# A hybrid encoder layer: the first output product of the attention beside the second pair's scores, and one k-tile in another order in three blocks

## The chip, the cores and the metric

The kernel runs on one core of a Trainium2 chip. A core has engines that work side by side, each with its own stream of instructions, and that wait for each other through semaphores: TensorE (PE in the profile; its weight loads are listed apart as PEld), VectorE (DVE), ScalarE (ACT), GpSimd (POOL), and SyncE (SP), which here only issues transfers. The metric is the device time of one execution in microseconds. A change of about 0.2% is what a measurement of this kernel can tell from none.

## What is computed

One layer of an encoder on a sequence of 256 tokens with a model width of 2048, all in 32-bit floats:

```python
hn = _rmsnorm(h, norm_w[i])
proj = hn @ w_in[i]
q, v, f_fwd, f_bwd, z_a, b_gate, c_gate, h_b, z_b = jnp.split(proj, IN_SPLITS, axis=-1)
o_a = _hgrn2_bidirectional(jax.nn.silu(q), v, f_fwd, f_bwd, lb_all[:, i])
o_a = _head_rmsnorm(o_a, hgrn_norm_w[i]) * jax.nn.silu(z_a)
y_b = b_gate * _short_conv(c_gate * h_b, conv_w[i])
o_b = _rmsnorm(y_b, conv_norm_w[i]) * jax.nn.silu(z_b)
h = h + jnp.concatenate([o_a, o_b], axis=-1) @ w_out[i]
gate = jax.nn.sigmoid(h @ w_ple_gate[i])
h = h + (p[i] @ w_ple[i]) * gate
return _rmsnorm(h, final_norm_w)
```

`_hgrn2_bidirectional` is a gated linear attention with 16 heads of 128, in chunks of 64 tokens, once forwards and once backwards: scores from `q` and `k`, masked, times `v`, with a decayed state carried from chunk to chunk.

## The kernel before

**Precision.** Each 32-bit operand is split into a high part in a faster format (`spl[..., 0]`, cast by ScalarE at L101) and the remainder (`spl[..., 1]`, subtracted by VectorE at L102). A product is then high x high, high x low and low x high. For the weights the two parts come from `Stream.split`, which runs three parts ahead of TensorE; a part holds four k-tiles of a block of 256 output columns, or less of a wider one. The weights arrive by transfers from SP into a ring of raw buffers.

**A block of the input projection.** `gemm_in(c, i, orders)` (L408) multiplies one block of 256 columns (two row tiles `m` of the transposed result) in 16 k-tiles. In one k-tile `gemm_part` (L393) issues four matmuls: for each `m` a long one (L403), whose moving operand has 512 columns, the high and the low part of the input side by side, against the weights' high part, and a short one (L401) with 256 columns against the weights' low part. The order is a table of pairs (m, short). `PLAIN` is long, short, long, short. `orders` gives single k-tiles another order: `SHORTS` is short, short, long, long, and `OUTER` is long, short, short, long. `ONE` puts `SHORTS` at k-tile 1, and `BOTH` puts `OUTER` at k-tile 1 and `SHORTS` at k-tile 5. All orders issue the same four matmuls.

**Ticks.** Each k-tile ends with `tick()` (L330), which counts up and runs what is due. `at(dt, fn)` (L297) puts `fn` in `dt` ticks from now. So work of the attention is issued between the k-tiles of projection blocks, on all engines at that place of the program. One block of `gemm_in` is 16 ticks.

**The attention half.** `two_pairs(i)` (L788) runs for i = 0, 2, 4, 6. Each call works on two pairs of heads, i and i + 1. It runs six blocks, `B_FF`, `B_FB` and `B_Q` for pair i and then for pair i + 1; then `gemm_vz` (L432), a product with 512 moving columns in every matmul, which gives `v` and `z` for both pairs (pair 0 uses the plainer `gemm_two`). `kicks` (L822) says which of the six blocks gets an order of its own. Four ticks into `gemm_vz` come the scores of pair i. What is put in after `gemm_vz` falls into the next call's first three blocks: the preparation of pair i + 1 at tick 4, `out(0)` at tick 12, the scores of pair i + 1 at tick 32 (at the end of the second block), `out(1)` at tick 46. In the first call, i = 0, `out(0)` and the scores of pair 1 are put in at one tick, in this order (L850, L851). After the last call, i = 6, the next blocks are those of the convolution half: `B_CG`, `B_HB` and `B_BG` of its loop (L901).

**What these steps issue.** The scores are 80 small matmuls (L711) and 8 of 128 columns (L755), then copies on VectorE and ScalarE and sums on POOL. `out(e)` (L842) calls `outputs` (L765): 16 matmuls as the profile counts them (L773, L774) into one PSUM bank (`o`, tag `y`), four squares with accumulated sums on ScalarE (L778) and one copy on VectorE (L779) into `ogz`, which `finish_two` reads at least 24 ticks behind the third block. `out(1)` uses the same bank as `out(0)`.

**The convolution half.** Eight rounds of four blocks (`B_CG`, `B_HB`, `B_BG`, `B_ZB`), all in plain order but for `B_BG` of round 0, which has `BOTH`. Meanwhile the output projection's weights are read and added up by transfers (`pump`). Then come the output projection and the gated embedding.

Of the kernel before, what the change touches and what calls it, by code (L numbers as in the profile page):

```python
# [25 lines left out]
B_Q, B_V, B_FF, B_FB, B_ZA, B_BG, B_CG, B_HB, B_ZB = (8 * i for i in range(9))  # L26
# [89 lines left out]
def tile_hymba_encoder(  # L116
# [180 lines left out]
    def at(dt, fn):  # L297
        pend.append((now[0] + dt, len(pend), fn))
# [91 lines left out]
    ONE = {1: SHORTS}  # L390
# [17 lines left out]
    def gemm_in(c, i, orders={}):  # L408

        acc = acc_in(c, i)  # L410
        for g in range(4):
            gemm_part(acc, ws.get(blocks[c, i][g]), g, orders=orders)
        return acc
# [374 lines left out]
    def two_pairs(i):  # L788
        vt = ap_.tile([P, 2, 512], F32, tag="vt", name=f"vt{i}")
        zt = ap_.tile([P, 2, 512], F32, tag="zt", name=f"zt{i}")  # L790
        ss = ap_.tile([P, 2, 2, 2], F32, tag="ss", name=f"ss{i}", bufs=2)
        ogs, steps, forgets = [], [], []
        before = last_two[0]
        if i == 6:
            for z in range(4):
                at(10 + 10 * z, lambda z=z: prepare(prepared[z]))
        else:


            todo = vz_prepared[i + 2]  # L800
            for z, what in enumerate(todo):
                at(50 + 10 * z, lambda what=what: prepare(what))
                for step in range(3):

                    dt = (166, 196, 220)[step] + z if i else 98 + 6 * step + z
                    at(dt, lambda what=what, step=step: add_up(what, step))
        if i == 2:

            def xsums(z):
                k = 2 * VZ_SUMS[z]  # L810
                a, t = xq[1][:, 0].rearrange("p (k t) -> p k t", k=2), xq[1][:, 1].rearrange("p (o t) -> p o t", o=4)
                act_sums(xs[:, k : k + 2], a, t)
                act_split(xq[0][:, z], xs[:, k : k + 2], t)

            for z in range(len(VZ_SUMS)):
                at(10 + 12 * z, lambda z=z: xsums(z))
        for e in range(2):
            xf = ap_.tile([P, 2, 2, T], F32, tag="xf", name=f"xf{i + e}", bufs=2)
            qt = ap_.tile([P, 2, T], F32, tag="qt", name=f"qt{i + e}")
            first3 = i + e == 0  # L820

            kicks = {(0, 1): ({}, ONE, BOTH), (2, 0): (ONE, BOTH, {}), (4, 0): ({}, {}, BOTH), (6, 0): ({}, {}, BOTH)}  # L822
            kick = kicks.get((i, e), ({}, {}, BOTH if i + e else {}))
            for j, (c, dst) in enumerate(((B_FF, xf[:, 0]), (B_FB, xf[:, 1]), (B_Q, qt))):

                acc, offset = acc3[j] if first3 else gemm_in(c, i + e, kick[j]), 500 if e and j == 2 else 200
                evac(acc, lambda m, dst=dst: dst[:, m, :], ap_, offset)

            def mix(e=e, xf=xf, qt=qt):
                forgets.append((xf, qt, mix_forgets(i + e, xf, qt)))  # L830
                if e == 0:
                    if before:
                        before()
                    steps.append(mix_pair(i, *forgets[0]))

            if first3:

                at(15, mix)
            else:
                mix()  # L840

        def out(e):  # L842
            ogs.append(ap_.tile([P, 2, 2, P], F32, tag="ogz", name=f"ogz{i + e}", bufs=2))
            steps[e][1](vt, ogs[e], ss[:, e])

        if i == 0:

            at(18, lambda: steps[0][0]())
            at(19, lambda: steps.append(mix_pair(i + 1, *forgets[1])))
            at(46, lambda: out(0))  # L850
            at(46, lambda: steps[1][0]())  # L851
            at(60, lambda: out(1))
            gemm_two(B_V, i, vt)
            xctx.close()
            xqp = xqctx.enter_context(tc.tile_pool(name="xqp", bufs=1, side="left", reuse_waits="tile"))
            xq.append(xqp.tile([P, len(VZ_SUMS), 4, 2, P], F32R, name="xsum"))
            xq.append(xqp.tile([P, 2, 512], F32, name="xd"))
            gemm_two(B_ZA, i, zt)
        else:

            at(4, lambda: steps[0][0]())
            gemm_vz(i, vt, zt)
            at(4, lambda: steps.append(mix_pair(i + 1, *forgets[1], here=True)))
            at(12, lambda: out(0))
            at(32, lambda: steps[1][0]())
            at(46, lambda: out(1))

        def rest():
            gate_two(i, zt)
            if i < 6:  # L870
                at(24, lambda: finish_two(ogs, ss, zt, ogs))
                for e in range(2):
                    at(32, lambda e=e: turn(i + e, ogs[e], "yx"[e]))
            else:

                def keep():
                    kept.extend(psm.tile([P, 2, 2, P], F32, tag=f"sc{e}", name=f"kept{e}") for e in range(2))
                    finish_two(ogs, ss, zt, kept)

                at(50, keep)  # L880

        last_two[0] = rest
# [17 lines left out]
    pool.memset(ysum, 0.0)  # L900
    for i in range(8):  # L901
        cg = ctmp.tile([P, 2, T], F32, tag="cg", name=f"cg{i}", bufs=2)
        evac(gemm_in(B_CG, i), lambda m: cg[:, m, :], ctmp)
        hb = ctmp.tile([P, 2, T], F32, tag="hb", name=f"hb{i}", bufs=2)
        evac(gemm_in(B_HB, i), lambda m: hb[:, m, :], ctmp)
        u = ub[i % 2]
        by_norms(cg, rbc2, 2)
        pump()
        pool.tensor_tensor(out=u[:, :, 1 : T + 1], in0=cg, in1=hb, op=ALU.mult)
        pump()  # L910
        for m in range(2):
            ct = 2 * i + m
            dve.tensor_scalar(cg[:, m, :], u[:, m, 0:T], cvw[:, 0, ct : ct + 1], None, op0=ALU.mult)
            for j in (1, 2):
                dve.scalar_tensor_tensor(
                    out=cg[:, m, :], in0=u[:, m, j : j + T], scalar=cvw[:, j, ct : ct + 1],
                    in1=cg[:, m, :], op0=ALU.mult, op1=ALU.add,
                )
        evac(gemm_in(B_BG, i, {} if i else BOTH), lambda m: hb[:, m, :], ctmp)
        pool.tensor_tensor(out=cg, in0=cg, in1=hb, op=ALU.mult)  # L920
        pump()
        y2 = ctmp.tile([P, 2, T], F32, tag="tmp", name=f"y2_{i}")
        act.activation(y2, cg, AF.Square)
        pool.tensor_tensor(out=ysum, in0=ysum, in1=y2, op=ALU.add)
        pump()
        evac(gemm_in(B_ZB, i), lambda m: hb[:, m, :], ctmp)
        by_norms(hb, rbc, 2)
        pump()
        sz = ctmp.tile([P, 2, T], F32, tag="tmp", name=f"szb{i}")
        act.activation(sz, hb, AF.Sigmoid)  # L930
        for m in range(2):
            ct = 2 * i + m
            dve.scalar_tensor_tensor(
                out=hb[:, m, :], in0=hb[:, m, :], scalar=cnw[:, ct : ct + 1], in1=sz[:, m, :],
                op0=ALU.mult, op1=ALU.mult,
            )
        pool.tensor_tensor(out=cg, in0=cg, in1=hb, op=ALU.mult)
        pump()
        if i == 0:
            assert not pend  # L940
            actx.close()
            bp = mctx.enter_context(tc.tile_pool(name="bp", bufs=1, side="right", reuse_waits="tile"))
            mixb = bp.tile([P, NH, 2, T], F32R, name="mixb")
            og = bp.tile([P, 2, 2, 2, P], F32, name="og")
            suma = bp.tile([P, len(SUMS), 3, 2, P], F32R, name="suma")
        if i == 2:
            for e in range(2):
                act.copy(out=og[:, e], in_=kept[e])
        hi, lo = mixb[:, 2 * i : 2 * i + 2, 0, :], mixb[:, 2 * i : 2 * i + 2, 1, :]
        act.copy(out=hi, in_=cg)  # L950
        dve.tensor_tensor(out=lo, in0=cg, in1=hi, op=ALU.subtract)
        for src, z, n in ((mixa, i - 1, len(SUMS)), (mixb, i - SUMS[0], len(sumb32))):
            if 0 <= z < n:
                k = 2 * SUMS[z]
                a = ctmp.tile([P, 2, T], F32, tag="tmp", name=f"sa{i}")
                if src is mixb:
                    act_sums(mixb[:, k : k + 2], a, sumb32[z])
                else:
                    t = ctmp.tile([P, 4, P], F32, tag="hb", name=f"sb{i}", bufs=2)
                    act_sums(mixa[:, k : k + 2], a, t)  # L960
                    act_split(suma[:, z], mixa[:, k : k + 2], t)
# [281 lines left out]
```

## Time and profile before

| | |
|---|---|
| runs | 1114.24, 1115.87, 1116.77 us (median 1115.87) |
| span of the profiled execution, first to last instruction | 1115.1 us |
| the profiled execution's own time | not given; its span lies within the runs |
| long matmuls (L403), 128x512 | 1792, mean length 395 ns |
| short matmuls (L401), 128x256 | 1792, mean length 280 ns |

The page gives the busy time of each engine, the span in 40 slices, the chain of work that ended last, and groups of instructions. Matmuls are pipelined: the length of one (395 ns) is longer than the distance to the next, so the rate is read from the starts of the rows in the timeline, not from the lengths. The timeline's rows give start, length, engine, line, operation, tiles and shape; a row with x3 merges three equal instructions in succession. In brackets stands the idle time of the engine before the row, and what ended it. The windows view gives, for a stretch, the busy time and the number of instructions of each engine, the granted clock of TensorE, the share of time that the transfer engines were busy, and GB/s. Pieces of the chain are start, length and what ran.

### The profile page before, as it was taken

How to read it: one execution, taken by the hardware profiler on the slowest of the kernel's cores; microseconds unless marked ns; L12 is line 12 of the kernel's file. 1: busy time of each engine (PE TensorE's matmuls, PEld its weight loads, DVE VectorE, ACT ScalarE, POOL GpSimd, SP SyncE). 2: the span in 40 equal slices, each digit the busy share in tenths (PEclk: the TensorE clock that was granted, in tenths of full speed). 3: DMA queues.
4: the chain of work that ended last, by engine and by line, in shares of the span. 5: the costliest groups of instructions: out<-in, count | busy, mean ns of one | idle time of the engine just before them, and what ended most of it. 6: DMA issues, size and time to landing. Idle time of an engine off the chain costs nothing.

```text
span 1115.1 us, 16970 instructions
## 1 busy us (share of the span) xinstructions
PE 1105.0 (99%) x6464; PEld 951.2 (85%) x6464; DVE 826.7 (74%) x1088; ACT 671.6 (60%) x939; POOL 291.5 (26%) x239
## 2 busy tenths in 40 slices
PE   9999999999999999999999999999999999999997
PEld 8888888888888888888888888888888888888886
DVE  7899467786887778797658748855758878877673
ACT  6787567666875697565535534534446565565562
POOL 1045325105530525043333223423331000000101
PEclk9999999999999999999999999999999999999998
DMA  9775985668778966858999998999979987887532
GB/s 348 273 249 192 223 266 179 217 227 213 234 207 306 303 172 182 279 180 206 296 312 252 263 335 218 294 311 266 298 201 296 332 287 284 297 305 254 196 132 76
DMA packets 79121, 277.76 MB, mean 249 GB/s; under 512 B 7872, under 2 KB 22080, under 8 KB 60736
## 3 DMA queue, kind: packets, MB, share of 16 engines
q1 hardware_dynamic: 64800, 253.26, 65.3%
q0 software_dynamic: 13952, 23.07, 13.6%
q8 instruction: 51, 0.84, 0.3%
q10 hardware_dynamic: 288, 0.34, 0.1%
q14 instruction: 30, 0.25, 0.1%
HBM read 274.55 MB, written 48.23 MB: 289 GB/s over the span
## 4 chain that ended last, share of the span: by engine, by line
PE 94%; ACT 2%; DMA 2%; POOL 1%; DVE 1%; issue 0%; DVEq 0%; ACTq 0%; POOLq 0%
PE a L403 34%; PE a L401 18%; PE avz L523 3%; PE avz L524 3%; PE avz L525 3%; PE pg L1004 3%; PE pg L1003 3%; PE pg L1005 3%; PE pa L523 2%; PE pa L524 2%; PE pa L525 2%; DMA raw<-in_w_in_dram 2%; PE a L424 1%; PE a L422 1%; PE a L423 1%; PE pb_sc L524 1%
## 5 line engine op out<-in xcount | busy, mean ns | idle before, releaser
L102 DVE TENSOR_TENSOR spl<-raw,spl 128x1024 fp32r<-128x1024 f32 (+2 forms) x413 | 505.7, 1238 | 190.1 <-ACT spl L101 187.5
L403 PE MATMUL a<-xs,spl 128*128 128x512 f32 x1792 | 624.6, 395 | 0.0
L101 ACT CAST spl<-raw 128x1024 fp32r<-128x1024 f32 (+2 forms) x413 | 409.0, 1001 | 250.6 <-PE a L401 88.1
L401 PE MATMUL a<-xs,spl 128*128 128x256 f32 x1792 | 496.8, 280 | 0.0
L403 PEld LDWEIGHTS a<-xs,spl 128*128 128x128 f32 x1792 | 334.6, 187 | 75.4
L401 PEld LDWEIGHTS a<-xs,spl 128*128 128x128 f32 x1792 | 337.5, 189 | 1.8
L1120 POOL TENSOR_TENSOR hh<-hh,fw 128x512 f32<-128x512 f32 (+1 forms) x9 | 11.0, 1228 | 250.7 <-ACT gt L1119 248.0
L523 PE MATMUL avz<-spl,xs 128*128 128x512 f32 x156 | 61.0, 391 | 0.6 <-DVE qt L464 0.6
L525 PE MATMUL avz<-spl,xs 128*128 128x512 f32 x156 | 60.7, 389 | 0.0
L524 PE MATMUL avz<-spl,xs 128*128 128x512 f32 x156 | 60.7, 389 | 0.0
L463 ACT COPY r<-a 128x256 f32<-128x256 f32 x112 | 40.4, 367 | 33.4 <-PE a L401 33.3
L692 POOL TENSOR_TENSOR qc<-pf,ge 128x256 f32<-128x256 f32 x16 | 23.2, 1453 | 106.5 <-ACT ge L679 95.6
L1003 PE MATMUL pg<-spl,ht 128*128 128x512 f32 (+1 forms) x120 | 45.2, 377 | 0.0
L1004 PE MATMUL pg<-spl,ht 128*128 128x512 f32 (+1 forms) x120 | 45.1, 376 | 0.0
L1005 PE MATMUL pg<-spl,ht 128*128 128x512 f32 (+1 forms) x120 | 45.0, 375 | 0.0
L468 POOL TENSOR_TENSOR xf<-xf,rbc 128x1024 f32<-128x1024 f32 x8 | 22.0, 2750 | 73.4 <-DVE rbc L379 49.4
L101 ACT CAST spl<-early 128x1024 fp32r<-128x1024 f32 (+1 forms) x29 | 28.7, 990 | 19.6 <-PE pb_y L525 7.5
L102 DVE TENSOR_TENSOR spl<-early,spl 128x1024 fp32r<-128x1024 f32 (+1 forms) x29 | 32.9, 1147 | 9.4 <-ACT spl L101 8.7
L920 POOL TENSOR_TENSOR cg<-cg,hb 128x512 f32<-128x512 f32 x8 | 14.6, 1826 | 80.6 <-DVE hb L464 80.6
L523 PEld LDWEIGHTS avz<-spl,xs 128*128 128x128 f32 x156 | 29.3, 188 | 6.9 <-DVE qt L464 0.8
L523 PE MATMUL pa<-spl,mixa 128*128 128x512 f32 x88 | 34.5, 392 | 0.0
L525 PEld LDWEIGHTS avz<-spl,xs 128*128 128x128 f32 x156 | 29.3, 188 | 6.1
(322 smaller groups left out, 1637.8 us busy)
## 6 DMA issues: line engine op xcount, KB each, us to landing
raw<-in_w_in_dram SPq DMA_DIRECT2D x106, 1024.0 KB, 7.4
raw<-in_w_in_dram SPq DMA_DIRECT2D x88, 256.0 KB, 4.1
raw<-in_w_out_dram SPq DMA_DIRECT2D x36, 512.0 KB, 5.2
sums<-in_w_out_dram SPq DMA_DIRECT2D x32, 512.0 KB, 11.4
raw<-in_w_in_dram SPq DMA_DIRECT2D x26, 512.0 KB, 7.0
raw<-sums SPq DMA_DIRECT2D x13, 1024.0 KB, 6.0
raw<-in_w_gate_dram SPq DMA_DIRECT2D x9, 1024.0 KB, 5.5
sums<-in_w_out_dram POOLq DMA_DIRECT2D x16, 512.0 KB, 10.0
```

The costliest lines, as they stand in the source:

```text
L101: self.nc.scalar.copy(out=v[:, :, 0], in_=r)
L102: self.nc.vector.tensor_tensor(out=v[:, :, 1], in0=r, in1=v[:, :, 0], op=ALU.subtract)
L401: pe.matmul(a[:, :T], lhsT=lhsT, rhs=xs[:, kt, 0, :], start=False, stop=(kt == NKT - 1))
L403: pe.matmul(a, lhsT=lhsT, rhs=xs[:, kt, :, :].rearrange("p s n -> p (s n)"), start=(kt == 0), stop=False)
L463: act.copy(out=r, in_=acc[m][:, 1, :])
L523: pe.matmul(acc, lhsT=ah, rhs=w[:, 0], start=start, stop=False)
L524: pe.matmul(acc, lhsT=ah, rhs=w[:, 1], start=False, stop=False)
L525: pe.matmul(acc, lhsT=al, rhs=w[:, 0], start=False, stop=stop)
L692: pool.tensor_tensor(out=c64(dst[:, d]), in0=c64(src[:, d, :, half * P : (half + 1) * P]), in1=g.unsqueeze(3).broadcast_to([P, 2, 2, CH]), ...
L1003: pe.matmul(acc[m], lhsT=lh, rhs=wh, start=(kt == 0), stop=False)
L1004: pe.matmul(acc[m], lhsT=lh, rhs=wl, start=False, stop=False)
L1005: pe.matmul(acc[m], lhsT=ll, rhs=wh, start=False, stop=(kt == nk - 1))
```

## The change

`out(0)`, the output product of the first pair, is put in at tick 32 and not at tick 12; it stands ahead of the second pair's scores, which are put in at the same tick. Three blocks, the first ones after each `gemm_vz`, get `ONE`: their k-tile 1 is issued as short, short, long, long.

```diff
-            kicks = {(0, 1): ({}, ONE, BOTH), (2, 0): (ONE, BOTH, {}), (4, 0): ({}, {}, BOTH), (6, 0): ({}, {}, BOTH)}
+            kicks = {(0, 1): ({}, ONE, BOTH), (2, 0): (ONE, BOTH, {}), (4, 0): (ONE, {}, BOTH), (6, 0): (ONE, {}, BOTH)}
...
-            at(12, lambda: out(0))
+            at(32, lambda: out(0))
             at(32, lambda: steps[1][0]())
             at(46, lambda: out(1))
...
-        evac(gemm_in(B_CG, i), lambda m: cg[:, m, :], ctmp)
+        evac(gemm_in(B_CG, i, {} if i else ONE), lambda m: cg[:, m, :], ctmp)
```

## The prediction

> **What bounds it now.** The first view is the page: its span, its busy shares and the chain that ended last.
>
> ```profile
> span 1115.1 us, 16970 instructions
> PE 1105.0 (99%) x6464; PEld 951.2 (85%) x6464; DVE 826.7 (74%) x1088; ACT 671.6 (60%) x939; POOL 291.5 (26%) x239
> PE 94%; ACT 2%; DMA 2%; POOL 1%; DVE 1%; issue 0%; DVEq 0%; ACTq 0%; POOLq 0%
> ```
>
> TensorE is busy 99% of the span and holds 94% of the chain; the granted clock, in the windows rows further down, is 1.00. The other engines' work is therefore worth what it makes TensorE wait. The second view, the waits of TensorE, has one wait inside the program, 0.6 us on `qt` (treated below). So nearly all that is left is the spacing of the matmuls themselves, and for that I read TensorE's timeline row by row (columns: start, length, engine, line, operation).
>
> The three stretches that the change touches run from the end of a `gemm_vz` to the start of the third block behind it. This is the first of them, with the windows view of the first and the third (columns: stretch, us, TensorE's busy time and instructions, granted clock, DMA):
>
> ```profile
> 238.79 0.39 PE L403 MATMUL a<-xs,spl 128*128 128x512 f32 x1
> 247.27 0.38 PE L773 MATMUL o<-vt,s 128*128 128x128 f32 x2
> 248.97 0.48 PE L403 MATMUL a<-xs,spl 128*128 128x512 f32 x1
> 263.27 0.30 PE L711 MATMUL scps<-qc,dd 128*32 128x128 f32 x2
> 265.46 0.47 PE L403 MATMUL a<-xs,spl 128*128 128x512 f32 x1
> ...
> 238.79:265.46 26.67, 26.67 (x233) 1.00 0.62 184
> 476.65:503.32 26.67, 26.67 (x233) 1.00 0.53 163
> ```
>
> Twelve k-tiles take 247.27 - 238.79 = 8.48 us, 0.707 us each; then `out(0)`, 20 k-tiles, the scores, and the third block starts at 265.46. The stretch takes 26.67 us in both rows, with the same 233 instructions; the middle one is the same program on the next pair, and I count it alike. Now the same kind of block where its second k-tile already runs in the order that the change gives to three more, `B_FF` of pair 2:
>
> ```profile
> 126.56 0.39 PE L403 MATMUL a<-xs,spl 128*128 128x512 f32 x1
> 127.14 0.52 PE L401 MATMUL a<-xs,spl 128*128 128x256 f32 x3
> 127.49 0.87 PE L403 MATMUL a<-xs,spl 128*128 128x512 f32 x3
> 128.66 0.40 PE L403 MATMUL a<-xs,spl 128*128 128x512 f32 x1
> 137.67 0.40 PE L403 MATMUL a<-xs,spl 128*128 128x512 f32 x1
> ```
>
> The merged x3 rows show short, short, long, long in k-tile 1. From 128.66 to 137.67 there are 13 k-tiles: 9.01 / 13 = 0.693 us each. The matmuls are the same and their operands lie alike, yet a k-tile takes 0.693 us in one place and 0.707 us in the other. **There are two rhythms, 13.4 ns per k-tile apart.** Each holds itself until something disturbs it, and a k-tile in another order can move the array from the slow one to the fast one. Stretches of the convolution half, where no order differs, agree: x146 matmuls (long and short by turns) in a fast 25 us, x143 in a slow one, both at clock 1.00.
>
> ```profile
> 575.00:600.00 25.00, 25.00 (x146) 22.05 (x145) 18.61 (x27) 13.50 (x20) 10.66 (x8) 1.00 0.88 237
> 800.00:825.00 25.00, 25.00 (x143) 21.69 (x142) 15.41 (x21) 11.26 (x14) 6.17 (x6) 1.00 0.86 245
> ```
>
> **The change part by part.** (1) *The reordered k-tile in three blocks.* `B_FF` of pairs 4 and 6 and `B_CG` 0 get what `B_FF` of pair 2 has. Both sorts of block follow 512-column matmuls without a gap, so I take its duration whole: 137.67 - 126.56 = 11.11 us for 16 k-tiles, the reordered one among them. The block behind it has no kick and stays fast: 16 x 0.693 = 11.09 us.
>
> (2) *`out(0)` moved from tick 12 to tick 32, ahead of `scores` of the second pair.* What moves are 16 matmuls with their loads, four squares with their sums on ScalarE and one copy on VectorE. It issues no DMA and nothing on POOL or SP, so it passes no queue of theirs; what it passes on PE are 20 k-tiles. Pair 0 already runs `out(0)` straight into the scores:
>
> ```profile
> 108.36 0.38 PE L773 MATMUL o<-vt,s 128*128 128x128 f32 x2
> 110.24 0.30 PE L711 MATMUL scps<-qc,dd 128*32 128x128 f32 x2
> 112.42 0.48 PE L422 MATMUL a<-spl,xs 128*128 128x512 f32 x1
> ```
>
> There it takes 1.88 us to the scores and these 2.18 us. Alone at tick 12 it takes 248.97 - 247.27 = 1.70 us, but the first long matmul after it is 0.08 us late (length 0.48 instead of 0.40) and the last k-tile ahead of the scores ends 0.09 us late (263.07 to 263.27 instead of 0.12). 1.70 + 0.08 + 0.09 = 1.87: the move costs nothing and gains nothing by itself.
>
> ```profile
> 263.07 0.28 PE L401 MATMUL a<-xs,spl 128*128 128x256 f32 x1
> ```
>
> New stretch: 11.11 + 11.09 + 1.88 + 2.18 = 26.26 us against 26.67. That is 0.41 us, **three times: 1.23 us**. The third block starts from the scores as before and has its own kick, so its rhythm should be as now.
>
> (3) *The moved work on the other engines.* The squares and the copy now come beside the scores' own copy.
>
> ```profile
> L778 ACT ACTIVATE jk<-o x8: 252/278/293, 250.6 to 278.6; 128x128 f32<-128x128 f32 x8
> L779 DVE COPY ogz<-o x2: 674/675/676, 255.2 to 280.8; 128x512 f32<-128x512 f32 x2
> 265.74 0.59 ACT L762 COPY sx<-cx 128x512 f32<-128x512 f32 x1 [1.04 <-PE cx L755]
> 269.09 1.06 ACT L590 ACTIVATE xf<-xf 128x1024 f32<-128x1024 f32 x1 [1.46 <-POOL xf L468]
> ```
>
> Four squares of 0.28 us with their sums are under 2 us; ScalarE stands idle 1.04 + 1.46 = 2.5 us there, waiting for the scores and for POOL. The copy is 0.67 us on VectorE, 74% busy. I cost both at nothing. Without that cover the weight casts queued behind them would come later by what is left over; the cast at 260.55 (next fence) waits 1.77 us for TensorE to free a buffer, so ScalarE is ahead of TensorE here and not behind it. `out(1)` needs the bank that `out(0)` used: 14 k-tiles and the scores, about 12 us, lie between, and pair 0 does the same without a wait. `ogz` is not read before tick 72.
>
> (4) *The one wait.* It stands at the next `gemm_vz`, where two banks are freed late.
>
> ```profile
> 262.89 16.82 DMA raw<-in_w_in_dram
> 279.79 1.05 ACT L101 CAST spl<-raw 128x1024 fp32r<-128x1024 f32 x1 [0.82 <-DMA raw<-in_w_in_dram]
> 260.55 1.05 ACT L101 CAST spl<-raw 128x1024 fp32r<-128x1024 f32 x1 [1.77 <-PE a L401]
> 316.79 1.16 PE L755 MATMUL cx<-qc,kx 128*128 128x128 f32 x8
> 318.58 0.50 PE L523 MATMUL avz<-spl,xs 128*128 128x512 f32 x1 [0.64 <-DVE qt L464]
> 436.14 1.16 PE L755 MATMUL cx<-qc,kx 128*128 128x128 f32 x8
> 437.11 0.50 PE L523 MATMUL avz<-spl,xs 128*128 128x512 f32 x1
> ```
>
> From the last score product group to the next matmul it is 1.79 us for pair 4 and 0.97 us for pair 6: 0.82 us lost. The chain leads back to a weight tile that landed at 279.79, for which ScalarE waited the same 0.82 us. That load was issued at 262.89, once the split of 260.55 had freed its buffer, and that split waited for TensorE, in the 13th k-tile of the second block. In the new order that k-tile starts at 238.79 + 11.11 + 12 x 0.693 = 258.22 instead of 260.35: 2.13 us earlier, since `out(0)` no longer lies ahead of it, while TensorE reaches the wait only 0.41 us earlier. That is 1.7 us more cover where 0.82 is short. Bounds: nothing gained (the landing is set by the other loads on the engines, not by the issue), or 0.82 us. I take 0.82, as the load has twice the cover that it lacks.
>
> **Sum:** 1.23 + 0.82 = 2.05 us. The page's span of 1115.1 becomes 1113.05. The runs shown are 1114.24 to 1116.77 with the median 1115.87, 0.8 above the span (the profiled execution's own time isn't given); on the median the sum gives **1113.8 us**.
>
> **The rivals.** *Rhythm alone.* The late landing stays late; only 1.23 us: 1114.6.
>
> *The kick doesn't take.* A reordered k-tile doesn't always reach the fast rhythm. This block (`B_Q` of pair 3) has two of them, and stays slow: 11.35 / 16 = 0.709.
>
> ```profile
> 182.87 0.48 PE L403 MATMUL a<-xs,spl 128*128 128x512 f32 x1
> 194.22 0.40 PE L523 MATMUL avz<-spl,xs 128*128 128x512 f32 x1
> ```
>
> Then both blocks stay at 0.707, the move is worth nothing, and the time stays 1115.9. For it speaks that phases of nanoseconds decide; against it, that the model block has the same neighbours before it. [...]
>
> *Slower: the slow rhythm returns earlier in the convolution half.* A split that ends late breaks the fast rhythm for good:
>
> ```profile
> 767.50 1.23 DVE L102 TENSOR_TENSOR spl<-raw,spl 128x1024 fp32r<-128x1024 f32 x1 [0.26 <-ACT spl L101]
> 768.78 0.19 PEld L401 LDWEIGHTS a<-xs,spl 128*128 128x128 f32 x1
> ...
> 769.90 0.24 PE a L403
> 838.80 0.24 PE a L403
> ...
> 585.32 1.21 DVE L102 TENSOR_TENSOR spl<-raw,spl 128x1024 fp32r<-128x1024 f32 x1
> 588.43 0.19 PEld L401 LDWEIGHTS a<-xs,spl 128*128 128x128 f32 x1
> ```
>
> The split ended at 768.73, a load of 768.69 came at 768.78, and from there to 838.80 the chain shows the slow rhythm's mark. At 588.43 the weights split at 585.32 to 586.53 were only 1.9 us early. If transfers fall 1.9 us later against TensorE there, the slow rhythm starts 181 us earlier: 181 / 0.693 x 13.4 ns = 3.5 us, less 1.23: 1118.1. Any loss of cover under 1.9 us doesn't do it.
>
> *Faster still.* If the split at 768.73 comes in time, the 70 us behind it run fast: 70 / 0.707 x 13.4 ns = 1.3 us more, 1112.5.
>
> **How the numbers follow.** Forecast 0.42, rhythm alone 0.22, kick fails 0.14, slower 0.07, faster still 0.15. About 0.2% (2.2 us) is what a measurement of this kernel can tell from no change: the bounds are 1113.6 and 1118.1. The forecast lies 0.2 us inside, and the runs spread by 2.5 us, so I give 0.16 of its 0.42 to faster. Faster: 0.15 + 0.16 + 0.01 of the second = 0.32; slower 0.06; the rest, 0.62, is within. The range goes from just under faster still to above the failed kick: 1112.3 to 1116.6.
>
> **What would show it.** The blocks behind the first two `gemm_vz` at 0.693 us per k-tile from the third one on, and 26.26 us per stretch, show (1) and (2); 26.67 refutes (1). 1.88 us from `out(0)` to the scores shows (2). About 0.97 us where 1.79 stands now shows (4). The prediction is wrong if the reordered k-tile lands in the slow rhythm, if the third block's kick fails after the new neighbour, or if the fast rhythm ends elsewhere than at 768.

## The result, and the profile after

| | before | after |
|---|---|---|
| median of 6 runs each, us | 1115.99 | 1125.59 |
| lowest and highest | 1114.24, 1116.77 | 1117.81, 1128.36 |
| span of the profiled execution | 1115.1 | 1124.0 |

The changed kernel is slower: ratio 1.0073, 95% interval 1.0053 to 1.0092. The forecast was 1113.8 with 1112.3 to 1116.6 as its range, so the time lies 9.0 us above the top of that range. Beside the experiments below, on five chips, the kernel before ran 106 times between 1114.23 and 1121.60 us, 25 times at 1119 or more, so the six runs above are not its whole spread; two single runs far outside (1573.66 and 2856.12) are left out of the ratios. What makes its upper runs, no profile shows. The profiled execution of after took 1125.76 us, 1.8 above its span. The page after, span, busy shares and chain:

```profile
span 1124.0 us, 16967 instructions
PE 1110.9 (99%) x6464; PEld 952.5 (85%) x6464; DVE 829.3 (74%) x1088; ACT 672.0 (60%) x937; POOL 281.9 (25%) x239
PE 92%; DVE 4%; ACT 2%; POOL 1%; issue 1%; DVEq 0%; POOLq 0%; ACTq 0%
```

TensorE is still busy 99%, but 2% of the chain has gone over from TensorE, and VectorE's share rose from 1% to 4%. Something other than matmul spacing now sets part of the time. The windows view places it (columns: stretch, us, busy time and instructions of PE, PEld, DVE, ACT and POOL, granted clock, DMA). The rows are the first and the third stretch of the prediction, the two groups of transposes (L634), the k-tiles behind the second group, and all projection blocks from `out(1)` of the last call to the end of the convolution half; the second fence has that last stretch and the second transposes before.

```profile
238.17:264.44 26.27, 26.27 (x234) 23.31 (x232) 23.25 (x33) 17.53 (x30) 12.06 (x10) 1.00 0.67 208
480.81:507.15 26.34, 26.34 (x234) 23.32 (x232) 25.64 (x30) 17.76 (x31) 12.46 (x9) 1.00 0.63 176
299.62:302.88 3.26, 1.45 (x11) 0.84 (x9) 3.26 (x8) 1.90 (x4) 0.00 (x0) 1.00 0.97 216
420.12:423.44 3.32, 1.44 (x10) 0.83 (x9) 3.32 (x8) 1.89 (x4) 0.00 (x0) 1.00 0.80 167
423.44:426.50 3.06, 3.06 (x11) 2.62 (x11) 3.06 (x5) 0.47 (x1) 0.20 (x1) 0.51 0.80 289
518.79:848.18 329.39, 329.39 (x1868) 285.71 (x1867) 218.99 (x293) 158.92 (x221) 106.15 (x89) 1.00 0.92 268
```

```profile
514.84:839.35 324.51, 324.51 (x1867) 285.11 (x1866) 217.35 (x293) 157.16 (x221) 108.81 (x89) 1.00 0.93 273
420.01:420.80 0.79, 0.79 (x10) 0.79 (x9) 0.79 (x2) 0.79 (x2) 0.79 (x1) 1.00 0.76 236
```

The difference of the two profiled spans, +8.9 us, is made up so:

| place | us |
|---|---|
| up to the first `gemm_vz` end | -0.62 |
| the three stretches, 26.67 to 26.27, 26.27 and 26.34 | -1.13 |
| the waits at the two later `gemm_vz` (1.79 and 0.97 to 0.91 and 0.91) | -0.93 |
| transposes before the third block of pairs 5 and 7, 0.79 to 3.26 and 3.32 | +5.00 |
| the block behind the second transposes, at half clock for 3 us | +1.53 |
| blocks from the third scores to the end of the convolution half | +5.00 |
| the rest | +0.06 |

The gains came as forecast: 1.13 + 0.93 = 2.06 us against 2.05. The three losses that the forecast did not have, 5.00 + 1.53 + 5.00 = 11.5 us, outweigh them more than fivefold.

**The transposes.** They turn the normed output of two pairs (`ogz`, scaled by `finish_two` from L624) for the output projection, as eight small matmuls. TensorE's timeline, after and then before:

```profile
299.62 0.49 PE L634 MATMUL ogt<-ident,ogz 128*128 128x128 f32 x3
300.59 0.59 PE L634 MATMUL ogt<-ident,ogz 128*128 128x128 f32 x2 [0.47 <-DVE ogz L624]
302.51 0.59 PE L634 MATMUL ogt<-ident,ogz 128*128 128x128 f32 x3 [1.33 <-DVE ogz L624]
```

```profile
300.65 1.04 PE L634 MATMUL ogt<-ident,ogz 128*128 128x128 f32 x8
```

Before, all eight run in a row; after, TensorE stands still twice, 1.33 us the second time, for VectorE's product into `ogz`. Why it is late stands in the timelines of ScalarE, GpSimd and VectorE after:

```profile
286.92 0.64 ACT L613 ACTIVATE sz<-zt 128x512 f32<-128x512 f32 x1 [0.78 <-POOL qt L593]
291.76 0.63 ACT L613 ACTIVATE sz<-zt 128x512 f32<-128x512 f32 x1
295.18 0.30 ACT L618 ACTIVATE ss<-ss,epst 128x8 f32<-128x8 f32 x1
```

```profile
293.61 1.92 POOL L698 TENSOR_TENSOR kx<-kc,ge 128x512 f32<-128x512 f32 x1
295.47 1.66 POOL L318 DMA_DIRECT2D vz<-vz  x2
296.56 1.90 POOL L614 TENSOR_TENSOR zt<-zt,sz 128x512 f32<-128x512 f32 x1
```

```profile
295.82 3.32 DVE L624 SCALAR_TENSOR_TENSOR ogz<-ogz,ss,zt 128x128 f32<-128x128 f32 x3
299.06 1.21 DVE L102 TENSOR_TENSOR spl<-raw,spl 128x1024 fp32r<-128x1024 f32 x1
300.20 0.60 DVE L624 SCALAR_TENSOR_TENSOR ogz<-ogz,ss,zt 128x128 f32<-128x128 f32 x2
300.72 1.21 DVE L102 TENSOR_TENSOR spl<-raw,spl 128x1024 fp32r<-128x1024 f32 x1
301.86 0.86 DVE L624 SCALAR_TENSOR_TENSOR ogz<-ogz,ss,zt 128x128 f32<-128x128 f32 x3
```

and before:

```profile
284.37 0.30 ACT L618 ACTIVATE ss<-ss,epst 128x8 f32<-128x8 f32 x1
288.96 0.64 ACT L613 ACTIVATE sz<-zt 128x512 f32<-128x512 f32 x1 [0.47 <-POOL qt L593]
```

```profile
294.09 1.66 POOL L614 TENSOR_TENSOR zt<-zt,sz 128x512 f32<-128x512 f32 x1 [1.57 <-ACT sz L613]
```

```profile
298.12 0.60 DVE L624 SCALAR_TENSOR_TENSOR ogz<-ogz,ss,zt 128x128 f32<-128x128 f32 x2
```

The order of the three engines' queues has changed, though the diff moved nothing there but four squares and a copy. The norm's square root (L618) ran before both sigmoids of the gate (L613) at 284.37 and now runs behind them at 295.18; GpSimd makes the gate's second product (L614) behind the mixing product `kx` and two transfers, at 296.56 instead of 294.09; and VectorE's eight products, done at 298.72 before, now end at 302.72, the last ones behind two weight splits. The likely reason lies in how the program is made: a planner orders each engine's queue by priorities that follow the place of an instruction in the program (raised where the source says `tc.high_priority`). The squares of `out(0)` feed the square root. Put in 20 ticks later, they let the planner place everything that follows from them later, on all engines. That the new order comes with the move, and that a higher priority undoes it, the runs below show (e2, e3); by which of its rules the planner arrived at it, no run shows.

**The convolution half.** Before, the fast rhythm held from the kick in the first `B_BG` to 768; after, the blocks run at 0.707 us per k-tile from the start to the end. The stretch has 466 k-tiles; 466 x 13.4 ns = 6.2 us between all fast and all slow, and before lost 1.3 of these. At the entry to that block, GpSimd's last score factor (`qc`) and TensorE's scores, after:

```profile
496.85 1.75 POOL L468 TENSOR_TENSOR cg<-cg,early 128x512 f32<-128x512 f32 x1
503.31 1.59 POOL L692 TENSOR_TENSOR qc<-pf,ge 128x256 f32<-128x256 f32 x1
```

```profile
504.96 0.11 PEld L711 LDWEIGHTS scps<-qc,dd 128*32 128x32 f32 x2 [0.19 <-POOL qc L692]
```

The factor ends at 504.90, so the scores start at 504.96, 1.94 us behind the start of `out(0)` instead of 1.88. The wait costs 0.06 us of TensorE's time, but the block behind it enters in another phase. The wait lets the slow rhythm in and does not always bring it: the profiles of e3, e4, e7 and e12 below have the same wait (1.94 to 1.97 us from `out(0)` to the scores), and in them the half starts fast.

### The profile page after: what moved, and what is told of

It reads as the page before. It is cut to its first block, busy times and chain, and to the rows that moved or that the text cites. A ratio compares the mean times of both kernels' runs of the same rounds, so it can differ in the third digit from the quotient of the medians.

```text
span 1124.0 us, 16967 instructions
## 1 busy us (share of the span) xinstructions
PE 1110.9 (99%) x6464; PEld 952.5 (85%) x6464; DVE 829.3 (74%) x1088; ACT 672.0 (60%) x937; POOL 281.9 (25%) x239
## 4 chain that ended last, share of the span: by engine, by line
PE 92%; DVE 4%; ACT 2%; POOL 1%; issue 1%; DVEq 0%; POOLq 0%; ACTq 0%
PE a L403 33%; PE a L401 17%; PE avz L523 3%; PE avz L525 3%; PE avz L524 3%; PE pg L1004 3%; PE pg L1005 3%; PE pg L1003 3%; PE pa L523 2%; PE pa L524 2%; PE pa L525 2%; PE a L422 1%; PE a L424 1%; PE a L423 1%; DVE spl L102 1%; PE pb_sc L525 1%
## 5 line engine op out<-in xcount | busy, mean ns | idle before, releaser
L102 DVE TENSOR_TENSOR spl<-raw,spl 128x1024 fp32r<-128x1024 f32 (+2 forms) x413 | 498.7, 1220 | 191.9 <-ACT spl L101 183.7
L692 POOL TENSOR_TENSOR qc<-pf,ge 128x256 f32<-128x256 f32 x16 | 26.7, 1670 | 117.2 <-ACT ge L679 104.5
L468 POOL TENSOR_TENSOR xf<-xf,rbc 128x1024 f32<-128x1024 f32 x8 | 20.8, 2600 | 88.7 <-DVE rbc L379 48.8
L523 PE MATMUL pa<-spl,mixa 128*128 128x512 f32 x88 | 34.5, 392 | 0.0
L524 PE MATMUL pa<-spl,mixa 128*128 128x512 f32 x88 | 34.4, 391 | 0.0
## 6 DMA issues: line engine op xcount, KB each, us to landing
sums<-in_w_out_dram POOLq DMA_DIRECT2D x16, 512.0 KB, 11.4
```

The lines of the kernel that those rows point to most:

```text
L102: self.nc.vector.tensor_tensor(out=v[:, :, 1], in0=r, in1=v[:, :, 0], op=ALU.subtract)
L523: pe.matmul(acc, lhsT=ah, rhs=w[:, 0], start=start, stop=False)
L524: pe.matmul(acc, lhsT=ah, rhs=w[:, 1], start=False, stop=False)
L692: pool.tensor_tensor(out=c64(dst[:, d]), in0=c64(src[:, d, :, half * P : (half + 1) * P]), in1=g.unsqueeze(3).broadcast_to([P, 2, 2, CH]), ...
```

## The experiments

In all of them theory A says that the new order of the other engines' queues makes the transposes late; theory B that the slow convolution half comes from the way in which the first `B_BG` is entered. Rivals stand with each expectation. Ratios are to the kernel before on the same chip.

**e1 and e2: each part of the change alone.** e1 has the new `kicks` and `ONE` in `B_CG`, with `out(0)` at tick 12; e2 is the converse.

```diff
-            at(32, lambda: out(0))
+            at(12, lambda: out(0))
```

> The three reordered k-tiles alone, out(0) left at tick 12. The queues of ScalarE, VectorE, POOL and SP hold the same instructions in the same order as before. Theory A (the move lets the planner put the queues of ScalarE, VectorE and POOL in another order, and TensorE then waits for the attention's products at its transposes): the transposes of pairs 4 and 6 take 0.79 us as before, the stretches about 26.3 us instead of 26.67, and the time is about 1.2 us under before (1114.8) if B_BG 0 lands in the fast rhythm, about 3.7 above it (1119.7) if it lands in the slow one. Theory B (the fast rhythm itself takes cover away from the other engines): the transposes take 2 us or more longer here too, and the time is above 1118.

> out(0) at tick 32 alone, all blocks in the order of before. The queues of ScalarE, VectorE, POOL and SP are those of the changed kernel. Theory A: the transposes of pairs 4 and 6 take about 3.3 us each instead of 0.79, one or both; the time is 4 to 7 us above before (1120 to 1123), more by 5 where the convolution half runs in the slow rhythm. Theory B: the transposes take 0.79 us and the time is that of before, 1116, within 1 us.

| | median, us | ratio | span |
|---|---|---|---|
| e1, orders alone | 1115.5 | 0.9985 (0.9975 to 0.9994) | 1113.6 |
| e2, move alone | 1123.68 | 1.0058 (1.0037 to 1.0080) | 1121.2 |

The windows of e1 (the first stretch; the wait at the second `gemm_vz`; the convolution half) and of e2 (the second transposes and the k-tiles behind them; the convolution half):

```profile
238.81:265.08 26.27, 26.27 (x233) 23.23 (x232) 22.25 (x32) 16.79 (x29) 10.75 (x10) 1.00 0.62 186
316.39:318.88 2.49, 1.16 (x17) 0.97 (x8) 2.04 (x5) 2.49 (x6) 0.00 (x0) 1.00 0.44 184
514.44:837.62 323.18, 323.18 (x1867) 284.96 (x1866) 218.97 (x293) 157.47 (x221) 109.55 (x89) 1.00 0.94 274
```

```profile
422.35:425.58 3.23, 1.45 (x10) 0.84 (x9) 3.23 (x8) 1.90 (x4) 0.00 (x0) 1.00 0.82 169
425.58:428.50 2.92, 2.92 (x11) 2.54 (x11) 2.92 (x5) 0.47 (x1) 0.06 (x1) 0.51 0.92 297
521.10:844.95 323.85, 323.46 (x1867) 284.95 (x1866) 216.05 (x293) 156.12 (x221) 112.75 (x89) 1.00 0.93 272
```

The orders alone bring the stretches from 26.67 to 26.27 and leave the transposes at 0.79; the other engines' queues are those of before, instruction by instruction. The move alone has the changed kernel's queues and its loss at the transposes. It also takes away the wait at `gemm_vz`, which e1 keeps and lengthens (2.49 us where before had 1.79). So the move brings both the gain of term (4) and the loss.

Neither profile has the slow convolution half: e1's is fast to the end (323.18), and e2's loses 0.7 us at one late weight split (e2's seven runs reach 1128.24, so the slow half may come there too, but no profile shows it). GpSimd's last factor and TensorE's scores in e2:

```profile
505.42 1.60 POOL L692 TENSOR_TENSOR qc<-pf,ge 128x256 f32<-128x256 f32 x1
```

```profile
507.39 0.30 PE L711 MATMUL scps<-qc,dd 128*32 128x128 f32 x2
```

The factor ended at 507.02, 0.37 us ahead of the scores. With the orders too, TensorE comes to the scores 0.4 us sooner, and the slack is used up. **The gain of one part spent the slack that the other had left.**

**e3: the norm early again.** The changed kernel, with a higher priority in the plan for `finish_two`.

```diff
-                at(24, lambda: finish_two(ogs, ss, zt, ogs))
+                def finish():
+                    with tc.high_priority(offset=300):
+                        finish_two(ogs, ss, zt, ogs)
+
+                at(24, finish)
```

> The changed kernel with finish_two of pairs 0 to 5 at a higher priority for the planner (offset 300): its square root on ScalarE stands again ahead of the sigmoids of the gates; out(0) stays at tick 32. Theory A: the transposes of pairs 4 and 6 take under 1.5 us; the time is 5 to 7 us under the changed kernel (about 1119), near 1114.5 where B_BG 0 lands in the fast rhythm. Theory C (out(0)'s own squares and copy are too late at tick 32, whatever the order behind them): the transposes still take about 3.3 us and the time stays near 1125.

Median 1114.2, ratio 0.9991 (0.9972 to 1.0009). The windows of both transposes:

```profile
300.39:301.18 0.79, 0.79 (x10) 0.79 (x9) 0.79 (x2) 0.79 (x2) 0.79 (x2) 1.00 0.00 0
418.44:419.23 0.79, 0.79 (x10) 0.79 (x9) 0.79 (x2) 0.79 (x2) 0.79 (x2) 1.00 0.00 0
```

The product stays at tick 32, the transposes are back at 0.79, and no half clock follows. The order was the cause, not the lateness of the product itself. The 12 runs fall into two levels: seven from 1112.51 to 1114.32, five from 1119.78 to 1120.70. The six runs of the changed kernel can be read so too (1117.81 and 1119.71 against 1125.41 to 1128.36).

**e12: the square root alone early.** The same priority for the square root, without the products.

```diff
-        act.activation(ss, ss, AF.Sqrt, bias=epst, scale=1.0 / P)
+        with tc.high_priority(offset=300):
+            act.activation(ss, ss, AF.Sqrt, bias=epst, scale=1.0 / P)
```

> The changed kernel with a higher priority in the plan for the norm's square root alone; the products of the norm keep theirs. In the plan that is enough for GpSimd too: the second gate product stands ahead of the mixing products again. Theory A (the place of the square root is what went wrong): transposes 0.79 to 1.3 us both times, no half-clock block, two levels as in e3, 1112.5 to 1114.5 and 1119 to 1121. Rival (the products' own late place on VectorE, behind the weight splits, is what makes TensorE wait, and e3 cured that): transposes 2 us and more, 1117 and more.

Neither was right in full. TensorE's timeline at the first transposes:

```profile
300.69 0.71 PE L634 MATMUL ogt<-ident,ogz 128*128 128x128 f32 x5
302.00 0.59 PE L634 MATMUL ogt<-ident,ogz 128*128 128x128 f32 x3 [0.60 <-DVE ogz L624]
```

Both groups take 1.68 us: of the 2.5 us lost at each, 1.6 belong to the place of the square root (with it the gate's second product on GpSimd comes back ahead, at 294.04), and 0.9 to the three last products behind one more weight split on VectorE. Median 1121.65, ratio 1.0034 (1.0017 to 1.0051), eight of the 12 runs in the upper level (1120.87 to 1123.41), four at 1116.18 to 1118.31.

**e5: a late norm without the move.** The kernel before, with the square root held behind the sigmoids.

```diff
-        act.activation(ss, ss, AF.Sqrt, bias=epst, scale=1.0 / P)
+        tc.keep_in_program_order(act.activation(ss, ss, AF.Sqrt, bias=epst, scale=1.0 / P))
...
-                at(24, lambda: finish_two(ogs, ss, zt, ogs))
+                at(26, lambda: finish_two(ogs, ss, zt, ogs))
```

> The kernel before, with the output product left at tick 12 and no new order in any block; the norm of two pairs is put in at tick 26 instead of 24 and its square root keeps its place in the program, which puts it on ScalarE behind both sigmoids of the gate and two exponentials, about where the planner put it in the changed kernel; GpSimd keeps nearly the order of before. Theory A (the late place of the square root makes the transposes of L634 wait, wherever the output product stands): the transposes of the pairs' groups take 2 to 3.5 us instead of 0.79, three times, and one or two of the blocks behind them run a few k-tiles at half clock (up to 1.6 us each); span 1121 to 1125, stretches 26.67 as before, convolution half 323 to 326. Rival theory D (what matters is GpSimd's order, the mixing products ahead of the gate's second product, not the square root): transposes at 0.79, span 1115.

Median 1134.28, ratio 1.015 (1.0127 to 1.0173). The windows of the three groups of transposes (in the first, matmuls of the next block are mixed in), then the waits of TensorE (what waited for what: us, times, longest):

```profile
184.92:193.17 8.25, 6.52 (x24) 5.20 (x24) 8.10 (x12) 0.65 (x2) 3.34 (x2) 0.61 0.32 98
308.48:313.43 4.95, 1.64 (x9) 0.86 (x8) 4.95 (x10) 2.83 (x5) 2.43 (x3) 0.96 1.00 247
432.72:436.87 4.15, 1.64 (x9) 0.83 (x8) 4.15 (x10) 2.01 (x5) 1.63 (x3) 0.89 0.97 245
```

```profile
PE ogt L634 <- DVE ogz L624: 10.2, 9, 2.7
```

The late square root, with the norm put in two ticks later, makes TensorE wait for the same product, with GpSimd's order nearly that of before: theory A again. The size was missed by 6 us, since the root came even later here: at 307.2 for the second group, with the first transpose at 308.48.

**e4: more kicks.** The changed kernel with `BOTH` in every `B_ZB`, to bring a slow convolution half back.

```diff
-        evac(gemm_in(B_ZB, i), lambda m: hb[:, m, :], ctmp)
+        evac(gemm_in(B_ZB, i, BOTH), lambda m: hb[:, m, :], ctmp)
```

> The changed kernel with BOTH in every B_ZB block of the convolution half; nothing else differs, the other engines' queues included. If the half is slow because its rhythm was lost at B_BG 0 and nothing brings it back, the stretch from the end of out(1) to the output product goes from 329.4 us to about 325, as soon as one of the eight blocks' kicks takes, and the time is about 4 to 5 us under the changed kernel (1121). If the loss there were waits for weights, it would stay at 329 and the time at 1125 to 1126.

Median 1121.45, ratio 1.0031 (1.0016 to 1.0045). In the profiled run the first `B_BG` entered fast anyway. Four windows of 25 us from its convolution half:

```profile
525.00:550.00 25.00, 25.00 (x144) 21.68 (x143) 16.72 (x22) 13.90 (x18) 9.70 (x8) 1.00 0.99 249
575.00:600.00 25.00, 25.00 (x147) 21.87 (x146) 18.18 (x26) 12.61 (x19) 8.60 (x6) 1.00 0.92 273
700.00:725.00 25.00, 25.00 (x144) 21.67 (x143) 18.76 (x26) 14.26 (x22) 10.89 (x8) 1.00 1.01 292
750.00:775.00 25.00, 25.00 (x146) 21.85 (x145) 13.20 (x17) 11.43 (x17) 10.95 (x8) 1.00 0.97 282
```

Slow, fast, slow, fast (x144 to x147 matmuls in a window): the kicks of the first and the fifth round lost the fast rhythm, those of the second and the sixth brought it back, the others left it as it was. A kick can move the array either way. The expectation that it leads to the fast rhythm was half wrong, and its time of 1121 came out in part by luck: this half was not slow to begin with, and lost 2.35 us to the two kicks and one short wait. What does speak for the expectation is that none of the ten runs lies above 1123.58.

**e6 and e7: where the two levels come from.** e6 is e3 with `out(0)` left at tick 12 in the last call, where GpSimd then has its old order; e7 is e3 without the kick of the first `B_BG`.

```diff
-            at(32, lambda: out(0))
+            at(32 if i < 6 else 12, lambda: out(0))
```

```diff
-        evac(gemm_in(B_BG, i, {} if i else BOTH), lambda m: hb[:, m, :], ctmp)
+        evac(gemm_in(B_BG, i, {}), lambda m: hb[:, m, :], ctmp)
```

> The changed kernel with the norm early (as in e3), but the output product of the last call stays at tick 12, so that GpSimd's last score factor is not behind the scores there and the convolution half is entered as in the kernel before. Theory B (the two levels of e3, 1112.5 to 1114.3 and 1119.8 to 1120.7, come from the kick of the first B_BG, which takes or fails by the entry that the wait for the last factor sets): all runs in one level, 1112 to 1114.5, the scores of the third stretch 1.70 to 1.88 behind the product, convolution half 323.2. Rival (the two levels come from elsewhere, such as the transfers): two levels again, some 6 us apart.

> e3 with the first B_BG in plain order. Theory B: the blocks behind the entry of the convolution half hold whatever rhythm they enter with; with no kick to move them all runs lie at one level, either near 1120 (slow from the entry on, convolution half 329 us, 0.707 us per k-tile) or near 1114 (fast). Since the third block after the scores starts slow in every profile (9.82 us for 14 k-tiles), slow is the likelier, 1119.5 to 1121. Rival (the levels come from elsewhere): two levels again as in e3.

e6: 12 runs from 1113.16 to 1116.93, one level; ratio 0.9969 (0.9956 to 0.9982). e7: two levels still, eight runs from 1112.80 to 1116.36 and four from 1119.08 to 1120.43; ratio 0.9989 (0.9971 to 1.0007). So the levels do not hang on the kick: in e7's profile the block stands in the fast rhythm from its second k-tile, with no kick. Theory B had the place right and the means wrong. What e6 takes away is the wait for the last factor; it also puts the product back to tick 12 there, which e8 and e9 below do not. Its half took 324.51 us, as in the kernel before, and not the 323.2 expected.

**e8 and e9: that wait alone.** e3, with a higher priority for the second pair's mixing products in the last call; the product stays at tick 32 everywhere. e9 is the same without the kick.

```diff
-            at(4, lambda: steps.append(mix_pair(i + 1, *forgets[1], here=True)))
+            def mix2():
+                with tc.high_priority(offset=200) if i == 6 else ExitStack():
+                    steps.append(mix_pair(i + 1, *forgets[1], here=True))
+
+            at(4, mix2)
```

> e3 with one more step: in the last call the mixing products of the second pair get a higher priority in the plan, so that GpSimd makes the last score factor ahead of the convolution half's first product and its transfer, and VectorE the product that it needs ahead of two weight splits. The output product stays at tick 32 in all three places. Theory B2 (the two levels of e3 and e7 come from the wait of the scores for that factor, which lets the next block enter in one of several phases): no wait, 1.88 us from the product to the scores in the third stretch, all 12 runs at one level, 1112 to 1114.5, convolution half 323.2. Rival (the levels come from the move itself or from elsewhere): two levels some 6 us apart again, 1113 and 1120.

> e8 with the first B_BG in plain order. Theory B2 with the kick as the means: without the wait the block enters as the third blocks of the other stretches do, whose first k-tiles stand in the slow rhythm until their kick; with no kick the convolution half then stays slow, 329 us, and all runs lie at 1119.5 to 1121. Rival (the block enters fast by itself, as in e7's profile): 1112 to 1114.5.

GpSimd and TensorE at the third scores in e8:

```profile
492.23 1.00 POOL L692 TENSOR_TENSOR qc<-pf,ge 128x256 f32<-128x256 f32 x1 [0.63 <-DVE pf L684]
```

```profile
497.02 0.38 PE L773 MATMUL o<-vt,s 128*128 128x128 f32 x2
498.90 0.30 PE L711 MATMUL scps<-qc,dd 128*32 128x128 f32 x2
```

The factor is done at 493.23, 5.7 us before it is read, and the scores follow `out(0)` at 1.88. The upper level of e3 is gone. e8: 1112.87 to 1118.22, median 1114.33, ratio 0.9973 (0.9958 to 0.9987). e9: 1112.51 to 1114.85 and one run at 1118.26, median 1113.88, ratio 0.9960 (0.9946 to 0.9975). The kick's part of the expectation for e9 was wrong: without the wait the block enters fast by itself. The 9.82 us for 14 k-tiles, read as a slow start in the expectation for e7, are one long first k-tile of 0.78 us and fast ones behind it. The runs at 1117 and 1118 and e6's upper end lie where a fast rhythm that ends part-way through the convolution half would put them (e9's profiled half took 324.95 us, slow in its last seven blocks; e8's 323.18). Those runs left no profile, so this is argued. e6, e8 and e9 are faster than both kernels, by 0.3 to 0.4% against the kernel before; which of them is best is within their intervals. A good part of that is spread: none of their 35 runs reaches 1119, while 15 of the 43 runs of the kernel before beside them do, although the last factor has 7 us of slack there. So the wait for it is what makes the levels of e3 and e7, and not the only thing that can cost several microseconds.

**e10 and e11: the same step in the changed kernel, beside the changed kernel again.** e10 is the changed kernel with e8's edit of `mix_pair` alone, the norm left late.

> The changed kernel with e8's second step alone: the last score factor early in the last call, the norm's square root left late. By both theories together (A: late square root, transposes wait twice; B2: the wait for the last factor lets the convolution half enter slow in some runs) the transposes still take 3.2 to 3.4 us each and the blocks behind them up to 1.6 us more, so about 1118.5 to 1122, but no run near 1126 to 1128, since the convolution half is fast (323.2 to 325). Rival (the slow convolution half hangs on the half-clock blocks or on the later time): runs near 1125 to 1128 as the changed kernel has.

> The changed kernel itself, to see its levels beside e10 on one chip. By B2 it has two levels some 6 us apart, about 1118 to 1121 and 1125 to 1128, as its six runs so far suggest (1117.81 and 1119.71 against 1125.41 to 1128.36). Rival: one spread without a gap.

e11: 1126.84, ratio 1.0074 (1.0048 to 1.0101), with one run at 1117.90 and six from 1124.33 to 1129.05; the gap is there, the lower level with a single run. e10: 1120.7, ratio 1.0033 (1.0018 to 1.0047), 1117.66 to 1125.64. The first transposes take 3.23 us in e10 as in the changed kernel, and the third scores come 1.88 us behind `out(0)`. The highest run, 1125.64, came close to the rival's 1125 to 1128, but without a gap below it. The convolution halves of the two profiles, e11 and then e10:

```profile
521.41:850.79 329.38, 329.38 (x1867) 285.51 (x1866) 216.82 (x293) 158.59 (x221) 107.05 (x89) 1.00 0.93 268
519.37:846.30 326.93, 326.77 (x1867) 285.26 (x1866) 217.49 (x293) 156.78 (x221) 108.78 (x89) 1.00 0.92 270
```

In e11 the half is slow from its entry, with 1.95 us from `out(0)` to the scores, as in the changed kernel. In e10 it enters fast, as B2 has it, but takes 326.93 us and not the 323.2 to 325 expected: at 685.01 a weight load waits 0.43 us for its split on VectorE, and from that block on a k-tile takes 0.707 us. So an early factor saves the entry, and the rhythm can still be lost later.

| medians, us | factor late | factor early |
|---|---|---|
| norm late | 1126.84 (e11) | 1120.7 (e10) |
| norm early | 1114.2 (e3, two levels) | 1114.33 (e8, one level) |

The two losses are separate, since each edit takes its own away. By the medians the order of the norm costs 1120.7 - 1114.33 = 6.4 us (on two chips; 0.6% by the ratios; the fast rhythm that e10's profile loses part-way is in it), and the wait for the last factor 1126.84 - 1120.7 = 6.1 us more, in most runs of the changed kernel.

## Why the prediction was wrong, step by step

**(1) The reordered k-tile: right.** 22.20 us for the 32 k-tiles of the first two blocks, as forecast (11.11 + 11.09), in all three stretches; 1.13 us in sum instead of 1.23, the missing part being mostly the third stretch's wait in (2). The rival "the kick doesn't take" did not come there.

**(2) The move on TensorE: right, with one exception.** 1.87 and 1.88 us from `out(0)` to the scores in the first two stretches. The third took 1.94, for a factor of GpSimd that the step did not look at. (Of its sum, the second delay is 0.08 by the rows, 263.27 - 263.07 - 0.12, and not 0.09; that changes nothing.)

**(3) The moved work on the other engines: this step failed.** It said: "I cost both at nothing", from four squares under 2 us in an idle time of 2.5 us, and "`ogz` is not read before tick 72". Both facts hold. What failed is what the step took for granted, that the queues of ScalarE, GpSimd and VectorE would keep their order, with only four squares and a copy put in elsewhere. They did not: the square root moved from ahead of the gate to behind it, and eight products that had ended 1.9 us ahead of the transposes (298.72 against 300.65) came up to 3.1 us behind their start. e3 and e5 show that this order alone makes the loss, with the move and without it. Where the step put nothing, the trace has +5.00 us of transposes, +1.53 us of half clock and, through the last factor (below), the +5.00 us up to the end of the convolution half.

**(4) The wait at `gemm_vz`: right.** It went from 1.79 to 0.91 us; e1 keeps it without the move, and e2 loses it with the move, so the move did it. The step's path fits: the load goes out at 260.14 in after and 260.56 in e2, against 262.89 before and 262.56 in e1, and ScalarE no longer waits for it (the cast of 279.41 in after). That the reordered queues had no part in it, no run shows.

**The slower rival** had the right kind of loss, the slow rhythm from early in the convolution half, by a wrong mechanism: a late split at 588. What came was the entry of the first `B_BG`. "The third block's kick fails after the new neighbour" was named among what would make the prediction wrong, but never priced. The working for it stood ready: 466 k-tiles x 13.4 ns less the 1.3 us already lost gives 4.9 us, and 4.88 was measured. The rival's rule that a late split ends the fast rhythm "for good" is too strong: in e2 a weight load waits 0.71 us for its split at 775.73, and the blocks behind it run at 0.693 us per k-tile all the same. Its counterpart, *faster still*, came in the experiments: in e1, e3, e7, e8 and e12 the half is fast to the end (323.18 or 323.19 us). Nor was the slack of the factor read. In the profile of before:

```profile
492.86 1.07 POOL L692 TENSOR_TENSOR qc<-pf,ge 128x256 f32<-128x256 f32 x1
```

```profile
501.13 0.30 PE L711 MATMUL scps<-qc,dd 128*32 128x128 f32 x2
```

It is done at 493.93 and read at 501.13, 7.2 us later. That shrank to nothing because GpSimd's order changed (the convolution half's `cg` at L468, a transfer and the product `kx` went ahead of it), the same oversight as in (3).

## What to carry to other kernels

Where a planner orders the queues by place in the program, a moved block of work can move its consumers on every engine: compare the instruction order of all engines before costing the rest at nothing. Read the slack of each producer ahead of the engine that bounds the time, and ask what is left of it if the bound gets faster. And where a rhythm holds itself, a wait of 0.06 us at the entry of a long stretch can cost by that stretch's length, and not by its own.

## What the hardware showed unasked

**Half clock without a long gap.** Behind the transposes the granted clock is 0.51 for 3 us (window 423.44:426.50), although the longest wait between two groups of them is 1.33 us. The Trainium skill, TensorE: Matmul & The Clock Gate, puts the drop to half clock after an idle window of about 3.4 us (section What's actually happening) and says that transposes do not count as busy in the same way (Part 4: PE-mode transpose). The two together fit: the stretch from the last projection matmul is 3.2 to 3.4 us long and holds nothing else. The Trainium skill also says there (What's actually happening) that the window runs freely and is not reset when a kernel starts. That would fit too, since the drop comes only some of the time: the block behind took 12.4 to 12.9 us instead of 11.2 to 11.4 after six of the ten such groups in after, e2, e4, e10 and e11, and after none of the groups of 0.79 or 1.68 us. In e5, where the groups take 4.15 to 8.25 us, the granted clock fell at all three: 0.61 over the first, 0.50 and 0.60 in the 3.1 us behind the others. No run tested it by itself.

**A rhythm can be lost and won by the same edit.** e4's kicks switched it four times in one execution, twice each way, and in plain order the first `B_BG` entered fast in the profiles of e7 and e9, while four runs of e7 lie at the upper level. What fixes the phase at an entry, in nanoseconds, stays open.
